# A two-layer attention and Fourier kernel: layer-1 conditioning moved to the gate stage, one reciprocal for both heads, the second low half behind the next maxima

## The chip, the cores and the metric

The kernel runs on one core of one Trainium2 chip. The metric is the device time of one execution in microseconds (us); the figure for a kernel is the median of its timed runs. The engines are TensorE (PE, with its weight loads shown apart as PEld), VectorE (DVE), ScalarE (ACT), GpSimd (POOL) and SyncE (SP), which here only issues DMAs.

## The reference, cut to what matters

Everything is fp32 in and out. Layer 0 is latent attention, layer 1 a Fourier mixing; both are conditioned by a vector.

```python
for i in range(2):
    sh, sc, gt = split(silu(c) @ w_ada[i] + b_ada[i], 3)      # conditioning: three thirds of 1024
    u = rms_norm(h, norm_g[i]) * (1 + sc) + sh
    if i == 0:      # 8 heads, 1024 queries, 1280 keys (256 of them context)
        s = q @ k.T * scale                # q, k from low-rank projections, rotary part added
        p = softmax(s)                     # max, exp, sum over 1280 keys
        y = ((p @ v) * silu(u @ w_gate)) @ w_out0
    else:
        y = (real(fft2(u @ w_z)) * silu(u @ w_gate1)) @ w_out1
    h = h + gt * y
out = rms_norm(h) * final_g
```

So layer 1 needs three vectors of 1024 numbers from `w_ada[1]` (a 1024 x 3072 matrix, 12 MB): `sh` and `sc` before its first product, `gt` at its end.

## The kernel before, in words

To keep fp32 accuracy each operand of a product is split in a high and a low part (`split`: ACT rounds the high part, DVE or POOL subtracts it), and three products are summed (`mm3`, L82).

Stages, by the time of the profiled execution: up to about 95 us the layer-0 conditioning, norms and projections; from 95 to 198 us the **gate stage**; from 198 to 548 us the **attention stage**; then the out-projection of layer 0 with the residual, and from about 600 us layer 1.

*Gate stage.* Nine turns `n`; turn 2 makes the rotary queries (`q_rope`), each other one a chunk of 128 gate columns for two blocks of 512 tokens (`gate_pair`: 2 x 24 matmuls, about 11 us). The weights of a chunk come by DMA on SP's queue into one raw tile `gr`, then ACT writes `gh` and POOL `gl` (L89, L90). Between the turns stand *conditioning thirds* (`ada_third`): a third is sixteen pieces of 128 x 512 of `w_ada`, each loaded by SP into `aw` (four buffers) or `qm` (two) and accumulated by DVE in `aacc` with one scalar_tensor_tensor (L467); POOL clears `aacc` first. `mod_rows` then sums over partitions with four matmuls by ones (L487), ACT copies the result and SP writes it to DRAM (`modd`). Before, two thirds (layer 0's `gt`, layer 1's `gt`) are done here, in turns 0 and 3.

*Attention stage.* 32 steps `i`; `u = i // 4` counts pairs of heads times two token blocks, `p = i % 4` the 128 queries. In a step PE makes the scores of two heads (`scores`, L618 and the last pass L624) in banks 0 to 2 and 3 to 5 of PSUM. `expo`: DVE takes the negated row maximum (L629), ACT the exponential with its sum (L631), into `p32`, which the profile calls `p`. `inverse` makes 1/sum times a power of two on DVE (L635, L636). One step later, in `between`, `quant` writes for each head the high half `hi` on ACT (L642), the low half `lo` on DVE (L644), and SP issues a transposing DMA for each (L643, L645) into `PT`. Two steps later (`LAG`) `pv_step` multiplies `PT` with the values, `values` applies them to the gate. Also in `between` stand preparations: `prep_q` in steps with `p` 0 and 1 (its split is `qh` on ACT, `ql` on DVE, L92 and L93), `prep_pe` (tile `A`), `prep_w`. Layer 1's `sh` and `sc` are accumulated here before: `cond` puts two DVE instructions in each of 16 of the steps 5 to 25, and `mod_rows(1)` in step 28.

The order on PE is written out by hand up to the end of the attention stage, on DVE and ACT in the attention stage; elsewhere a scheduler that simulates the engines decides.

Of the kernel before, what the change touches and what calls it, by code (L numbers as in the profile page):

```python
# [12 lines left out]
ALU = mybir.AluOpType  # L13
# [20 lines left out]
NORM1 = {4: 4, 5: 6}  # L34
TOKENS1 = {6: (0, 1, 2), 7: (3, 4, 5, 6, 7)}

THIRDS = {0: (0, 0, 2), 3: (0, 1, 2)}
SUMS = {5: 0}

COND = [i for i in range(5, 27) if i % 4 != 2][:16]  # L40


def f32(ap):
# [3 lines left out]
def hybrid_kernel(tc, io, out, dbg=None):  # L47
# [384 lines left out]
    close(wq_cm)  # L432


    stb_cm, stb = pool("stb", "right")
    gws.append((stb.tile([P, 8, P], F32R, name="gh1"), stb.tile([P, 8, P], F32R, name="gl1")))

# [17 lines left out]
                cs = slice(e * 512, (e + 1) * 512)  # L455
                split(flat(w[0])[:, cs], flat(w[1])[:, cs], wr[:, cs], scale=gqa[:, e:e + 1])

    def ada_start(layer, j, pl):
        a = pl.tile([P, D], F32, name="aacc", tag="aacc", bufs=2)
        nc.gpsimd.memset(a, 0.0)  # L460
        nc.sync.dma_start(a[0:1, :], io["b_ada"][layer:layer + 1, j * D:(j + 1) * D])
        return a
# [4 lines left out]
        return stt(a[:, cs], w, actc[:, k, 0:1], a[:, cs], ALU.mult, ALU.add)  # L467

    def ada_third(layer, j, qmp=None):
        a = ada_start(layer, j, stb)  # L470
# [11 lines left out]
    def mod_rows(pair, pl):  # L482
# [5 lines left out]
        row = pl.tile([P, 512], F32, name="row", tag="row", bufs=1)  # L488
# [42 lines left out]

    def at(n):
        if n in SUMS:
            mod_rows(SUMS[n], qmp)
        if n in THIRDS:
            pair, layer, j = THIRDS[n]
            thirds.setdefault(pair, []).append(ada_third(layer, j, qmp if n > 2 else None))
# [86 lines left out]
                mm(s[d][:, a:z], qa[u % 2][1][d][x, q], (B1 if d else B2)[x, a:z], start=False, stop=True)  # L624
        return [v[:, 0:1280] for v in s]

    def expo(s):
        mx = atq.tile([P, 4], F32, name="mx", tag="mx", bufs=4)
        nc.vector.tensor_reduce(mx[:, 0:1], s, axis=AX, op=ALU.max, negate=True)  # L629
        p32 = atq.tile([P, 1280], F32, name="p32", tag="p32", bufs=2)  # L630
        act(p32, s, AF.Exp, bias=mx[:, 0:1], accum_out=mx[:, 1:2])  # L631
        return mx, p32

    def inverse(mx, p32):
        nc.vector.reciprocal(mx[:, 2:3], mx[:, 1:2])  # L635
        ts(mx[:, 3:4], mx[:, 2:3], PS14, None, ALU.mult)  # L636

    def quant(mx, p32, PT, half):
        r = mx[:, 3:4]
        hi = ptp.tile([P, 1280], F16, name="phi", tag="phi", bufs=2)  # L640
        lo = ptp.tile([P, 1280], F16, name="plo", tag="plo", bufs=2)
        act(hi, p32, AF.Copy, scale=r)  # L642
        nc.sync.dma_start_transpose(PT[0][:, half], hi)  # L643
        stt(lo, p32, r, hi, ALU.mult, ALU.subtract)  # L644
        nc.sync.dma_start_transpose(PT[1][:, half], lo)  # L645

    PTs, Os = {}, {}

    def pv_step(i, b=7):
        u, p = i // 4, i % 4  # L650
# [18 lines left out]
    gate_chunk(8, 0)  # L669
    for d in range(2):  # L670
        prep_q(0, d, (7, 5)[d])
    close(u_cms[0])
    pt_cm, ptp = pool("ptp2", "left")
    wo0 = [None] * 8
    wraw = [qpe[:, 2 * i:2 * i + 2, :].rearrange("p a c -> p (a c)") for i in range(4)]

    def cond(i, c):
        if i in COND:
            n = COND.index(i)
            w = cnp.tile([P, 512], F32, name="aw", tag="aw", bufs=2)  # L680
            ada_step(1, n // 8, thirds[1][n // 8], n % 8, c, w)

    def between(i):

        u, p = i // 4, i % 4
        if i > 0:
            for d in range(2):
                quant(*es[d], PTs[i - 1], d)
        if 0 < u < 7 and p < 2:
            prep_q(u + 1, p)  # L690
        if i == 2:
            prep_q(1, 1)
        if i == 3:
            prep_pe(1)
        if u > 0 and p == 2:
            values(u - 1, 0)
        if u in (0, 2, 4) and p == 3:
            prep_w(u // 2 + 1)
        if i in (2, 4):
            hs = slice(2 * i - 4, 2 * i)  # L700
            split(wvh[:, hs, :], wvl[:, hs, :], wvr[:, hs, :], scale=gkva)
        if i == 28:
            mod_rows(1, cnp)
        if i >= 29:
            split_wo0(i - 29)
        if i == 31:
            for t in range(2):
                o_split(t, slice(0, 4), wop, gtt)

    ots = [None] * 8  # L710

    def o_split(t, ks, pl, eng, bufs=4):
        if ots[t] is None:
            ots[t] = [None, None]
        sl = slice(t * P, (t + 1) * P)
        for q in range(ks.start // 4, (ks.stop + 3) // 4):
            if ots[t][q] is None:
                ots[t][q] = [pl.tile([P, 4, P], F32R, name=f"o{x}", tag=f"o{x}", bufs=bufs) for x in "hl"]
# [11 lines left out]
    for i in range(16 * 2):  # L730
        u, p = i // 4, i % 4
        if i == 5:
            close(wv_cm)
        if i == COND[0]:
            cn_cm, cnp = pool("cnp", "left")
            thirds[1] = [ada_start(1, j, cnp) for j in range(2)]
        PTs[i] = [ptp.tile([P, 2, NKT, P], F16, name="PT", tag=f"PT{j}", bufs=2) for j in range(2)]
        es = [expo(s) for s in scores(u, p, lambda: between(i))]
        cond(i, 0)
        for e in es:  # L740
            inverse(*e)
        if i < 2:
            gate_chunk(8, 1, range(4 * i, 4 * i + 4))
        if i == 1:
            close(u_cms[1])
            at_cm, atp = pool("atp", "left")
            qa.append(q_tiles(atp, 1))
            scr = atp.tile([P, 8], F32, name="scr")
            wvh, wvl = gws[0]
            wv_cm, wvp = pool("wvp", "left")  # L750
            wvr = wvp.tile([P, NH, P], F32, name="wvr")
            nc.gpsimd.dma_start(wvr, io["wv"])
            prep_q(1, 0, 7)
        if i >= LAG:
            pv_step(i - LAG)
        if 0 < u < 7 and p == 2:
            prep_pe(u + 1)
        if u > 0 and p == 3:
            values(u - 1, 1)
        cond(i, 1)  # L760
        if i == 27:
            for k in range(4):
                nc.gpsimd.dma_start(wraw[k], io["w_out0"][k * P:(k + 1) * P, :])  # L763
        if i == 28:
            close(cn_cm)
            for n, v in ((2, sh1), (3, scr)):
                nc.gpsimd.dma_start(v, modd[n].rearrange("(k p) -> p k", p=P))
            close(cq_cm)
            close(wqk_cm)
            wo_cm, wop = pool("wop", "right")  # L770
            for k in range(3):
                wo0[k] = [(wop.tile([P, 512], F32R, name=f"wh{k}{i_}"), wop.tile([P, 512], F32R, name=f"wl{k}{i_}")) for i_ in range(2)]
    for d in range(2):
        quant(*es[d], PTs[i], d)

    def out_mm(t, bs, ks, wo, first, last, beside=None):
        for k in ks:
# [14 lines left out]
        values(7, d, 4 + d)  # L792
    order2.__exit__(None, None, None)
    order.__exit__(None, None, None)
    for t in range(2):
        o_split(t, slice(4, 8), wop, gtt)
    in_order(stt(sc1, scr, 1.0, ng[:, 8:16], ALU.add, ALU.mult))
    dump("gate", gate)
    close(at_cm)
    close(pt_cm)  # L800
# [66 lines left out]
    for t in range(8):  # L867
        if t >= 2:
            bs = banks(2, 0, 2)
            beside = (lambda k: to_u2(0, n1[0:4], (k,))) if t == 5 else None  # L870
            out_mm(t, bs, range(8), wo0, 0, 7, beside)
        else:
            bs = b0[t]
        if t + 2 < 8:
            xts.append(load_res(t + 2))
            o_split(t + 2, slice(0, 8), wop, gtt)
# [440 lines left out]
```

## Time and profile before

| | us |
|---|---|
| timed runs | 903.22, 904.62, 908.70 |
| median | 904.62 |
| profiled execution | 902.2, its span 900.4 |
| PE busy in the span | 859.6 (95%) |
| DVE / ACT / POOL busy | 584.5 / 405.5 / 274.8 |

Busy time of PE is modelled: matmuls overlap, and a matmul of 512 columns that the profile gives 0.39 us follows its predecessor after 0.23 us. What tells is where PE stood idle and who released it. Times in the views are counted from the start of the span. TensorE runs at one of two levels, 2.4 GHz (granted clock 1.00) and 1.2 GHz (0.50); a value between is a mean over the stretch.

### The profile page before, as it was taken

How to read it: one execution, taken by the hardware profiler on the slowest of the kernel's cores; microseconds unless marked ns; L12 is line 12 of the kernel's file. 1: busy time of each engine (PE TensorE's matmuls, PEld its weight loads, DVE VectorE, ACT ScalarE, POOL GpSimd, SP SyncE). 2: the span in 40 equal slices, each digit the busy share in tenths (PEclk: the TensorE clock that was granted, in tenths of full speed). 3: DMA queues.
4: the chain of work that ended last, by engine and by line, in shares of the span. 5: the costliest groups of instructions: out<-in, count | busy, mean ns of one | idle time of the engine just before them, and what ended most of it. 6: DMA issues, size and time to landing. Idle time of an engine off the chain costs nothing. (4 is left out here: it accounts for less than half of the span.)

```text
span 900.4 us, 13245 instructions
## 1 busy us (share of the span) xinstructions
PE 859.6 (95%) x4963; PEld 709.8 (79%) x4963; DVE 584.5 (65%) x1058; ACT 405.5 (45%) x695; POOL 274.8 (31%) x249
## 2 busy tenths in 40 slices
PE   4999999999899999999999989999999999999996
PEld 2878877887777878787887767888888889988885
DVE  4366887016788888888888753453398736396644
ACT  4465521226656666566655653332343326342211
POOL 2544453200000000000000445764277625256311
PEclk9999999999999999999999999999999999999999
DMA  8921455105678878989989994312044315641221
GB/s 345 333 98 48 135 171 187 48 1 106 112 169 163 177 152 160 176 161 174 207 164 189 170 189 179 118 48 94 28 177 137 127 59 197 215 168 66 93 94 48
DMA packets 200729, 127.90 MB, mean 142 GB/s; under 512 B 171915, under 2 KB 175692, under 8 KB 200408
## 3 DMA queue, kind: packets, MB, share of 16 engines
q1 hardware_dynamic: 198632, 119.10, 51.7%
q0 software_dynamic: 2032, 7.95, 2.9%
q8 instruction: 39, 0.64, 0.3%
q14 instruction: 26, 0.21, 0.1%
HBM read 72.51 MB, written 12.57 MB: 94 GB/s over the span
## 5 line engine op out<-in xcount | busy, mean ns | idle before, releaser
L631 ACT ACTIVATE p<-pb,mx 128x1280 f32<-128x1280 f32 x64 | 85.1, 1329 | 103.4 <-DVE mx L629 103.1
L82 PE MATMUL pb<-PT,n16h 128*128 128x256 f16 x640 | 108.7, 276 | 3.7 <-DMA PT<-plo 3.7
L644 DVE SCALAR_TENSOR_TENSOR plo<-p,mx,phi 128x1280 f16<-128x1280 f32 x64 | 96.7, 1551 | 10.0 <-ACT phi L642 8.6
L629 DVE TENSOR_REDUCE mx<-pb 128x1 f32<-128x1280 f32 x64 | 92.3, 1483 | 8.3 <-PE pb L624 8.0
L82 PE MATMUL pb<-PT,n16l 128*128 128x256 f16 x320 | 88.0, 275 | 0.0
L642 ACT ACTIVATE phi<-p,mx 128x1280 f16<-128x1280 f32 x64 | 83.6, 1358 | 0.1
L82 PEld LDWEIGHTS <-n16h 128*128 128x128 f16 x640 | 60.5, 99 | 15.1 <-issue 8.0
L763 POOL DMA_DIRECT2D qpe<-w_out x4 | 2.1, 532 | 225.9 <-PE pb L596 225.9
L618 PE MATMUL pb<-nkh,qh 128*128 128x512 f32 (+1 forms) x192 | 50.9, 373 | 7.6 <-ACT p L631 7.5
L82 PE MATMUL pb<-wl,oh 128*128 128x512 f32 x128 | 50.1, 392 | 1.1 <-DVE wl L90 1.0
L467 DVE SCALAR_TENSOR_TENSOR aacc<-aw,actc,aacc 128x512 f32<-128x512 f32 x59 | 48.5, 832 | 3.7 <-DMA aw<-w_ada 3.5
L82 PE MATMUL pb<-uh,gh 128*128 128x512 f32 x128 | 50.7, 396 | 0.0
L82 PE MATMUL pb<-ul,gh 128*128 128x512 f32 x128 | 50.0, 391 | 0.0
L82 PE MATMUL pb<-uh,gl 128*128 128x512 f32 x128 | 49.9, 390 | 0.0
L82 PE MATMUL pb<-wh,ol 128*128 128x512 f32 x128 | 49.9, 390 | 0.0
L90 POOL TENSOR_TENSOR ol<-gate,oh 128x512 fp32r<-128x512 f32 (+2 forms) x28 | 41.5, 1493 | 27.6 <-ACT oh L89 26.4
L82 PE MATMUL pb<-wh,oh 128*128 128x512 f32 x128 | 48.7, 397 | 0.0
L618 PE MATMUL pb<-nkh,ql 128*128 128x512 f32 (+1 forms) x192 | 48.3, 360 | 0.0
L618 PE MATMUL pb<-B,A 128*128 128x512 f32 (+1 forms) x192 | 48.1, 359 | 0.0
L618 PE MATMUL pb<-nkl,qh 128*128 128x512 f32 (+1 forms) x192 | 47.7, 357 | 0.0
L618 PEld LDWEIGHTS pb<-nkh,qh 128*128 128x128 f32 x192 | 32.8, 190 | 18.3 <-ACT p L631 13.2
L89 ACT ACTIVATE oh<-gate 128x512 fp32r<-128x512 f32 (+2 forms) x36 | 19.2, 577 | 56.2 <-PE pb L82 50.8
(332 smaller groups left out, 2233.7 us busy)
## 6 DMA issues: line engine op xcount, KB each, us to landing
aw<-w_ada SPq DMA_DIRECT2D x59, 256.0 KB, 3.1
wada<-wada SPq DMA_DIRECT2D x16, 512.0 KB, 8.8
gr<-wg SPq DMA_DIRECT2D x14, 512.0 KB, 3.6
xn<-x SPq DMA_DIRECT2D x8, 512.0 KB, 5.0
xt<-x SPq DMA_DIRECT2D x8, 512.0 KB, 6.3
h1d<-xt SPq DMA_DIRECT2D x8, 512.0 KB, 2.6
wz<-wz SPq DMA_DIRECT2D x8, 512.0 KB, 3.7
ht<-h1d SPq DMA_DIRECT2D x8, 512.0 KB, 6.5
```

The costliest lines, as they stand in the source:

```text
L82: mm(ps, l, r, start=start and i == 0, stop=stop and i == n - 1)
L89: act(hi, src, AF.Copy)
L90: eng(lo, src, f32(hi), ALU.subtract)
L467: return stt(a[:, cs], w, actc[:, k, 0:1], a[:, cs], ALU.mult, ALU.add)
L618: mm(s[d][:, a:z], l[:, q], r[:, a:z], start=i == 0, stop=False)
L629: nc.vector.tensor_reduce(mx[:, 0:1], s, axis=AX, op=ALU.max, negate=True)
L631: act(p32, s, AF.Exp, bias=mx[:, 0:1], accum_out=mx[:, 1:2])
L642: act(hi, p32, AF.Copy, scale=r)
L644: stt(lo, p32, r, hi, ALU.mult, ALU.subtract)
L763: nc.gpsimd.dma_start(wraw[k], io["w_out0"][k * P:(k + 1) * P, :])
```

## The change

1. Conditioning: layer 1's `sh` and `sc` thirds go to turns 5 and 6 of the gate stage (`THIRDS`); `cond` is gone. The accumulators sit in a pool of their own (`smp`). `mod_rows(1)` comes right before the first scores; the result is loaded back by two DMAs on POOL's queue there.
2. Softmax: the maxima and sums of both heads share one tile `mx` of eight columns, and one reciprocal and one scaling serve both heads.
3. Order: the low half of the second head is not made in `between` but after the next step's two maxima (`lows`); `p32` has three buffers.
4. The second half of the first two output tiles (`o_split`, columns 4 to 8) is made after the pool `wo2` has been opened, and `sc1` is finished later.

```diff
-THIRDS = {0: (0, 0, 2), 3: (0, 1, 2)}
+THIRDS = {0: (0, 0, 2), 3: (0, 1, 2), 5: (1, 1, 0), 6: (1, 1, 1)}
 SUMS = {5: 0}
-COND = [i for i in range(5, 27) if i % 4 != 2][:16]
...
-    def expo(s):
-        mx = atq.tile([P, 4], F32, name="mx", tag="mx", bufs=4)
-        nc.vector.tensor_reduce(mx[:, 0:1], s, axis=AX, op=ALU.max, negate=True)
-        p32 = atq.tile([P, 1280], F32, name="p32", tag="p32", bufs=2)
-        act(p32, s, AF.Exp, bias=mx[:, 0:1], accum_out=mx[:, 1:2])
-        return mx, p32
-    def inverse(mx, p32):
-        nc.vector.reciprocal(mx[:, 2:3], mx[:, 1:2])
-        ts(mx[:, 3:4], mx[:, 2:3], PS14, None, ALU.mult)
+    def expo(s, mx, d):
+        nc.vector.tensor_reduce(mx[:, d:d + 1], s, axis=AX, op=ALU.max, negate=True)
+        p32 = ptp.tile([P, 1280], F32, name="p32", tag="p32", bufs=3)
+        act(p32, s, AF.Exp, bias=mx[:, d:d + 1], accum_out=mx[:, 2 + d:3 + d])
+        return p32
+    def inverse(mx):
+        nc.vector.reciprocal(mx[:, 4:6], mx[:, 2:4])
+        ts(mx[:, 6:8], mx[:, 4:6], PS14, None, ALU.mult)
...
         act(hi, p32, AF.Copy, scale=r)
-        nc.sync.dma_start_transpose(PT[0][:, half], hi)
-        stt(lo, p32, r, hi, ALU.mult, ALU.subtract)
-        nc.sync.dma_start_transpose(PT[1][:, half], lo)
+        nc.sync.dma_start_transpose(PT[0][:, d], hi)
+        def low():
+            stt(lo, p32, r, hi, ALU.mult, ALU.subtract)
+            nc.sync.dma_start_transpose(PT[1][:, d], lo)
+        if late:
+            return low
+        low()
...
     for d in range(2):
         prep_q(0, d, (7, 5)[d])
+    mod_rows(1, thirds[1][0][:, 0:512])
+    close(sm_cm)
+    for n, v in ((2, sh1), (3, sc1)):
+        nc.gpsimd.dma_start(v, modd[n].rearrange("(k p) -> p k", p=P))
...
-            for d in range(2):
-                quant(*es[d], PTs[i - 1], d)
+            quant(mx, es[0], PTs[i - 1], 0)
+            lows.append(quant(mx, es[1], PTs[i - 1], 1, True))
...
-        if i == 28:
-            mod_rows(1, cnp)
...
-        es = [expo(s) for s in scores(u, p, lambda: between(i))]
-        cond(i, 0)
-        for e in es:
-            inverse(*e)
+        ss = scores(u, p, lambda: between(i))
+        mx = atq.tile([P, 8], F32, name="mx", tag="mx", bufs=3)
+        es = [expo(s, mx, d) for d, s in enumerate(ss)]
+        while lows:
+            lows.pop()()
+        inverse(mx)
...
-        cond(i, 1)
...
-    for t in range(2):
-        o_split(t, slice(4, 8), wop, gtt)
-    in_order(stt(sc1, scr, 1.0, ng[:, 8:16], ALU.add, ALU.mult))
...
     wo2_cm, wo2 = pool("wo2", "right")
+    opl.append(wo2)
+    for t in range(2):
+        o_split(t, slice(4, 8), gtt)
...
     close(key_cm)
+    in_order(stt(sc1, sc1, 1.0, ng[:, 8:16], ALU.add, ALU.mult))
```

How instructions move, at three places (rows in the order of the engine; x2 is a row twice). First DVE in the attention stage, from the maxima of step 7 to those of step 8: before, then in the changed kernel.

```order
L629 TENSOR_REDUCE mx<-pb 128x1 x2
L467 SCALAR_TENSOR_TENSOR aacc<-aw,actc,aacc 128x512
L635 RECIPROCAL mx<-mx 128x1
L636 TENSOR_SCALAR mx<-mx 128x1
L635 RECIPROCAL mx<-mx 128x1
L636 TENSOR_SCALAR mx<-mx 128x1
L93 SCALAR_TENSOR_TENSOR Ol<-pb,Oh 128x2x128
L665 TENSOR_TENSOR gate<-pb,gate 128x512
L467 SCALAR_TENSOR_TENSOR aacc<-aw,actc,aacc 128x512
L644 SCALAR_TENSOR_TENSOR plo<-p_2601,mx,phi 128x1280
L644 SCALAR_TENSOR_TENSOR plo<-p_2605,mx,phi 128x1280
L93 SCALAR_TENSOR_TENSOR ql_2024<-pb,gks,qh_2023 128x512
```

```order
L627 TENSOR_REDUCE mx<-pb 128x1 x2
L645 SCALAR_TENSOR_TENSOR plo<-p_2584,mx,phi 128x1280
L633 RECIPROCAL mx<-mx 128x2
L634 TENSOR_SCALAR mx<-mx 128x2
L91 SCALAR_TENSOR_TENSOR Ol<-pb,Oh 128x2x128
L669 TENSOR_TENSOR gate<-pb,gate 128x512
L645 SCALAR_TENSOR_TENSOR plo<-p_2676,mx,phi 128x1280
L91 SCALAR_TENSOR_TENSOR ql_2132<-pb,gks,qh_2131 128x512
```

One low half (of the step before) now stands between the maxima and the reciprocal, one is left ahead of the next maxima; the two conditioning instructions and one reciprocal pair are gone.

Second SP's queue in the gate stage, from the last loads of the third in turn 3: before (the last row is the attention stage's first transpose), then in the changed kernel as far as the next gate weights but one.

```order
L466 DMA aw<-w_ada 128x512 x2
L449 DMA gr<-wg 128x1024
L490 DMA modd<-row 4x512
L449 DMA gr<-wg 128x1024 x2
L643 DMA_TRANSPOSE PT<-phi 128x10x128 x2
```

```order
L465 DMA aw<-w_ada 128x512 x4
L448 DMA gr<-wg 128x1024
L465 DMA aw<-w_ada 128x512 x2
L465 DMA qm<-w_ada 128x512
L488 DMA modd<-qm 4x512
L460 DMA aacc<-b_ada 1x1024
L465 DMA qm<-w_ada 128x512
L448 DMA gr<-wg 128x1024
L465 DMA aw<-w_ada 128x512
L460 DMA aacc<-b_ada 1x1024
```

The `gr` loads now stand between loads of `aw` and `qm`, each of which waits for a buffer that DVE has to free. On DVE all 32 new accumulations stand before the split of `wq` that opens the attention stage.

Third ACT at the end of the attention stage, from the last two high halves: before, then in the changed kernel.

```order
L642 ACTIVATE phi<-p_5049,mx 128x1280
L89 ACTIVATE oh<-gate 128x512 x2
L92 ACTIVATE Oh<-pb 128x2x128 x2
L89 ACTIVATE wh_5229<-qpe 128x512
L89 ACTIVATE wh_5231<-qpe 128x512
```

```order
L641 ACTIVATE phi<-p_4951,mx 128x1280
L90 ACTIVATE Oh<-pb 128x2x128 x2
L87 ACTIVATE oh<-gate 128x512 x2
L87 ACTIVATE wh_5130<-qpe 128x512
L87 ACTIVATE wh_5132<-qpe 128x512
```

The two high halves of the output tiles come behind the last attention results, ahead of the weights of the out-projection.

## Rows read from the trace of the kernel before

**Rows 1.** Waits of PE, 195 to 565 us: engine, line, waited for, us, times, longest

```profile
PE pb L618 <- ACT p L631: 7.5, 11, 2.2
```

**Rows 2.** Timeline of PE, attention stage: start us, us, what; in brackets idle before, releaser

```profile
229.29 0.84 PE L618 MATMUL pb<-nkh,qh 128*128 128x512 f32 x3 [2.24 <-ACT p L631]
...
281.49 0.39 PE L82 MATMUL pb<-Oh,gl 128*128 128x512 f32 x1
...
282.14 0.85 PE L618 MATMUL pb<-nkh,qh 128*128 128x512 f32 x3 [0.26 <-ACT p L631]
...
292.95 0.85 PE L618 MATMUL pb<-nkh,qh 128*128 128x512 f32 x3 [0.32 <-ACT p L631]
...
323.57 0.85 PE L618 MATMUL pb<-nkh,qh 128*128 128x512 f32 x3 [0.67 <-ACT p L631]
...
516.79 0.85 PE L618 MATMUL pb<-nkh,qh 128*128 128x512 f32 x3 [1.12 <-ACT p L631]
...
540.51 0.27 PE L82 MATMUL pb<-PT,n16h 128*128 128x256 f16 x1 [3.67 <-DMA PT<-plo]
...
550.27 0.50 PE L82 MATMUL pb<-wl,oh 128*128 128x512 f32 x1 [1.05 <-DVE wl L90]
```

**Rows 3.** Timeline of DVE in step 7: low halves, maxima, second reciprocal

```profile
276.04 3.02 DVE L644 SCALAR_TENSOR_TENSOR plo<-p,mx,phi 128x1280 f16<-128x1280 f32 x2
279.08 2.89 DVE L629 TENSOR_REDUCE mx<-pb 128x1 f32<-128x1280 f32 x2
...
283.52 0.16 DVE L635 RECIPROCAL mx<-mx 128x1 f32<-128x1 f32 x1 [0.62 <-ACT p L631]
```

**Rows 4.** Timeline of DVE before the maxima of step 8

```profile
289.23 0.75 DVE L93 SCALAR_TENSOR_TENSOR ql<-pb,gks,qh 128x512 fp32r<-128x512 f32 x1 [0.84 <-ACT qh L92]
```

**Rows 5.** Timeline of DVE before the maxima of step 2

```profile
224.30 0.74 DVE L93 SCALAR_TENSOR_TENSOR gl<-wvr,cols,gh 128x512 fp32r<-128x512 f32 x1
224.96 2.88 DVE L629 TENSOR_REDUCE mx<-pb 128x1 f32<-128x1280 f32 x2
```

**Rows 6.** Timeline of ACT: first split of wq, and qh of step 2

```profile
190.12 0.72 ACT L89 ACTIVATE wqh<-wqk 128x256 fp32r<-128x256 f32 x2
...
221.82 0.69 ACT L92 ACTIVATE qh<-pb,gks 128x512 fp32r<-128x512 f32 x1
```

**Rows 7.** Windows: length, busy PE PEld DVE ACT POOL, granted clock, DMA share, GB/s

```profile
230.00:235.00 5.00, 5.00 (x22) 4.32 (x21) 3.56 (x5) 4.50 (x7) 0.00 (x0) 0.66 0.36 69
500.00:520.00 20.00, 18.88 (x126) 15.32 (x125) 14.70 (x20) 13.46 (x19) 8.79 (x7) 1.00 0.99 185
```

**Rows 8.** Timeline of DVE, gate stage: conditioning accumulations

```profile
121.90 2.87 DVE L467 SCALAR_TENSOR_TENSOR aacc<-aw,actc,aacc 128x512 f32<-128x512 f32 x1 [0.51 <-DMA aw<-w_ada]
...
135.29 5.27 DVE L467 SCALAR_TENSOR_TENSOR aacc<-aw,actc,aacc 128x512 f32<-128x512 f32 x3
...
149.39 2.73 DVE L467 SCALAR_TENSOR_TENSOR aacc<-aw,actc,aacc 128x512 f32<-128x512 f32 x4
...
153.95 1.54 DVE L467 SCALAR_TENSOR_TENSOR aacc<-aw,actc,aacc 128x512 f32<-128x512 f32 x2
```

**Rows 9.** Timeline of POOL, gate stage: a low half of gate weights

```profile
168.71 2.41 POOL L90 TENSOR_TENSOR gl<-gr,gh 128x1024 fp32r<-128x1024 f32 x1 [8.78 <-ACT gh L89]
```

**Rows 10.** Timeline of SP: sums of layer 0 to DRAM; last low halves' transposes

```profile
158.41 0.59 SPq L490 DMA_DIRECT2D modd<-row  x1
...
532.63 3.30 SPq L645 DMA_TRANSPOSE PT<-plo  x2
```

**Rows 11.** Timeline of PE: first use of wq; sums of layer 1

```profile
195.37 0.39 PE L82 MATMUL pb<-cqh,wqh 128*128 128x512 f32 x1
...
492.05 1.06 PE L487 MATMUL pb<-aacc,ones 128*32 128x512 f32 x8
```

**Rows 12.** Timeline of DVE at the end of attention

```profile
548.94 0.67 DVE L797 SCALAR_TENSOR_TENSOR sc<-scr,cols 128x8 f32<-128x8 f32 x1
```

**Rows 13.** Tile PT, SP, 480 to 545 us

```profile
DMA to landing us min/median/max: 3.4/3.9/5.7
```

More of the change, by code (lines that the diff above doesn't have):

```diff
@@ L432, in hybrid_kernel @@
     close(wq_cm)
+    sm_cm, smp = pool("smp", "right")
     stb_cm, stb = pool("stb", "right")
@@ L456, in gate_w0, with ada_start @@
                 split(flat(w[0])[:, cs], flat(w[1])[:, cs], wr[:, cs], scale=gqa[:, e:e + 1])
-    def ada_start(layer, j, pl):
-        a = pl.tile([P, D], F32, name="aacc", tag="aacc", bufs=2)
+    def ada_start(layer, j):
+        a = smp.tile([P, D], F32, name="aacc", tag="aacc", bufs=2)
         nc.gpsimd.memset(a, 0.0)
@@ L469, in ada_third @@
     def ada_third(layer, j, qmp=None):
-        a = ada_start(layer, j, stb)
+        a = ada_start(layer, j)
         for k in range(8):
@@ L480, in ada_third, with mod_rows @@
         return a
-    def mod_rows(pair, pl):
+    def mod_rows(pair, row):
         b = bank(1, 5, 6, 7) if pair == 0 else pb[:, 6, :]
@@ L487, in mod_rows @@
             mm(b[32 * c:32 * c + 32, :], ones[:, 0:32], a, start=True, stop=True)
-        row = pl.tile([P, 512], F32, name="row", tag="row", bufs=1)
         act(row, b, AF.Copy)
@@ L533, in at @@
         if n in SUMS:
-            mod_rows(SUMS[n], qmp)
+            mod_rows(SUMS[n], qmp.tile([P, 512], F32, name="qm", tag="qm", bufs=2))
         if n in THIRDS:
@@ L625, in scores, with quant @@
         return [v[:, 0:1280] for v in s]
-    def expo(s):
-        mx = atq.tile([P, 4], F32, name="mx", tag="mx", bufs=4)
-        nc.vector.tensor_reduce(mx[:, 0:1], s, axis=AX, op=ALU.max, negate=True)
-        p32 = atq.tile([P, 1280], F32, name="p32", tag="p32", bufs=2)
-        act(p32, s, AF.Exp, bias=mx[:, 0:1], accum_out=mx[:, 1:2])
-        return mx, p32
-    def inverse(mx, p32):
-        nc.vector.reciprocal(mx[:, 2:3], mx[:, 1:2])
-        ts(mx[:, 3:4], mx[:, 2:3], PS14, None, ALU.mult)
-    def quant(mx, p32, PT, half):
-        r = mx[:, 3:4]
+    def expo(s, mx, d):
[6 more added lines that the diff above has]
+        ts(mx[:, 6:8], mx[:, 4:6], PS14, None, ALU.mult)
+    def quant(mx, p32, PT, d, late=False):
+        r = mx[:, 6 + d:7 + d]
         hi = ptp.tile([P, 1280], F16, name="phi", tag="phi", bufs=2)
@@ L642, in quant @@
         act(hi, p32, AF.Copy, scale=r)
-        nc.sync.dma_start_transpose(PT[0][:, half], hi)
-        stt(lo, p32, r, hi, ALU.mult, ALU.subtract)
-        nc.sync.dma_start_transpose(PT[1][:, half], lo)
-    PTs, Os = {}, {}
+        nc.sync.dma_start_transpose(PT[0][:, d], hi)
[5 more added lines that the diff above has]
+        low()
+    PTs, Os, lows = {}, {}, []
     def pv_step(i, b=7):
@@ L675, in hybrid_kernel @@
     wraw = [qpe[:, 2 * i:2 * i + 2, :].rearrange("p a c -> p (a c)") for i in range(4)]
[L677 to L681, printed above, removed]
     def between(i):
@@ L707, in between, with o_split @@
             for t in range(2):
-                o_split(t, slice(0, 4), wop, gtt)
+                o_split(t, slice(0, 4), gtt)
     ots = [None] * 8
-    def o_split(t, ks, pl, eng, bufs=4):
+    opl = []
+    def o_split(t, ks, eng):
         if ots[t] is None:
@@ L717, in o_split @@
             if ots[t][q] is None:
-                ots[t][q] = [pl.tile([P, 4, P], F32R, name=f"o{x}", tag=f"o{x}", bufs=bufs) for x in "hl"]
+                ots[t][q] = [opl[q].tile([P, 4, P], F32R, name=f"o{x}", tag=f"o{x}", bufs=2) for x in "hl"]
             oh, ol = ots[t][q]
@@ L733, in hybrid_kernel @@
             close(wv_cm)
-        if i == COND[0]:
-            cn_cm, cnp = pool("cnp", "left")
-            thirds[1] = [ada_start(1, j, cnp) for j in range(2)]
         PTs[i] = [ptp.tile([P, 2, NKT, P], F16, name="PT", tag=f"PT{j}", bufs=2) for j in range(2)]
-        es = [expo(s) for s in scores(u, p, lambda: between(i))]
-        cond(i, 0)
-        for e in es:
-            inverse(*e)
+        ss = scores(u, p, lambda: between(i))
[4 more added lines that the diff above has]
+        inverse(mx)
         if i < 2:
@@ L747, in hybrid_kernel @@
             qa.append(q_tiles(atp, 1))
-            scr = atp.tile([P, 8], F32, name="scr")
             wvh, wvl = gws[0]
@@ L764, in hybrid_kernel @@
         if i == 28:
-            close(cn_cm)
-            for n, v in ((2, sh1), (3, scr)):
-                nc.gpsimd.dma_start(v, modd[n].rearrange("(k p) -> p k", p=P))
             close(cq_cm)
@@ L770, in hybrid_kernel @@
             wo_cm, wop = pool("wop", "right")
+            opl.append(wop)
             for k in range(3):
@@ L773, in hybrid_kernel @@
     for d in range(2):
-        quant(*es[d], PTs[i], d)
+        quant(mx, es[d], PTs[i], d)
     def out_mm(t, bs, ks, wo, first, last, beside=None):
@@ L875, in hybrid_kernel @@
             xts.append(load_res(t + 2))
-            o_split(t + 2, slice(0, 8), wop, gtt)
+            o_split(t + 2, slice(0, 8), gtt)
         n1.append(residual(t, bs, xts[t]))
```

## The prediction

> **What bounds the kernel now.** I read first who kept PE waiting in the attention stage, since PE works without a gap nearly everywhere else. Eleven waits, 7.5 us together, end with the exponential of the first head [rows 1]: PE can start the next step's scores only when ACT has read the old ones out of PSUM. Then I read PE's timeline for the size of each. The largest are 2.24 us in step 2, 1.12 in step 30, and 0.67, 0.26 and 0.32 in steps 11, 7 and 8 [rows 2]; the row of step 11 stands for step 19 too, that of step 8 for steps 12, 16, 20 and 24, and a wait of 0.98 follows step 4. The other large one is not of that kind: 3.67 us until the last transposed low half has landed, and then 1.05 us for a low half of output weights [rows 2].
>
> Third I asked what held up the exponential. It waits for the maximum, so the question is what DVE did just before the maxima. There are two kinds of step. In step 7 the two low halves run from 276.04 to 279.06 and the maxima follow at 279.08 [rows 3]: the second low half is in their way. In step 8 the maxima come after `ql`, and DVE stood idle 0.84 us before `ql`, waiting for `qh` [rows 4]: there the way leads from PE's preparation over ACT, and no low half lies on it.
>
> A wait costs a little more than its idle time. In step 7 the last matmul before it starts at 281.49 and the next at 282.14, 0.65 us instead of about 0.23, so 0.42 us are lost and not 0.26 [rows 2]: 0.16 more each.
>
> **The change part by part.**
>
> *The low half behind the maxima* gains where it was what the maxima waited for. Steps 7, 11, 19 and 30: 0.26 + 0.67 + 0.67 + 1.12 = 2.72 us, with 4 x 0.16 = 0.64 that makes 3.4. A low half takes half of 3.02 us [rows 3], more than each of these waits, so they go entirely. In steps 8, 12, 16, 20, 24 and 4 `ql` is late for another reason: no gain. Step 2 lies between. After its low halves come `ql` and `gl` (0.74 us at 224.30), then the maxima at 224.96 [rows 5]. Without the second low half `ql` can start when `qh` is done, at 221.82 + 0.69 = 222.5 [rows 6]; two instructions of about 0.7 later the maxima start at 223.9, so 1.0 of 2.24 us goes.
>
> *Clock.* After the 2.24 us the granted clock was 0.66 in 230 to 235 us, a mean of 1.2 and 2.4 GHz; 5 x 0.34 = 1.7 us of work were lost. After 1.12 us idle the stretch 500 to 520 kept 1.00 [rows 7]. With 1.2 us left in step 2 I take the nearer row: no fall, gain 1.7 us. The bounds are 0 and 1.7.
>
> *What becomes late next.* The second low half now ends 4.45 us after its step's maxima begin (2.89 for the maxima, then 1.55), and its transpose lands 3.4 to 5.7 us after issue [rows 3, 13]: 7.9 to 10.2 us. `pv_step` needs it when the next step's scores end, about 10.2 us after the maxima in most steps (279.08 to 289.9 in step 7), under 9 in step 30. In most steps that is covered; in step 30 a wait of up to 1.2 us is possible, but PE then waits for the final transpose anyway.
>
> *One reciprocal for both heads.* DVE already stood idle 0.62 us until the second exponential's sum was there [rows 3], and the first high half follows that exponential on ACT. So it starts at most one reciprocal and one scaling (0.16 us each) later, which nothing waits for except at the end. It saves 64 tiny instructions off the path: nothing.
>
> *The end of attention.* The last transposes were issued from 532.63 over 3.30 us [rows 10]. Before them now lie the later reciprocal (0.3 us) and, close ahead on SP's queue, the transpose of step 30's second low half (1.65 us by the same row) in a stretch where the DMA engines are 0.99 busy [rows 7]. Bounds: 0.3 and 2.0 us of loss. I take 0.8, since SP would be free again at about the time when the first high half of step 31 is ready. On the other side `sc1` (0.67 us, [rows 12]) no longer stands before the first `wl` for which PE waited 1.05: gain 0.6. The output tiles' high halves now delay the weights of POOL's part by some 2.5 us, but those products were moved back on PE as well: between 0 and 1.5 us of loss, I take 0.
>
> *Conditioning.* Removing 32 DVE instructions of some 0.74 us from attention gains nothing by itself: they stood after the maxima or before a low half that waited for ACT. `mod_rows(1)` costs PE 1.06 us at 492 [rows 11] and will cost that at 198: nothing. What must be found is room in the gate stage. Accumulation can start when layer 0's sums have left: `modd` is issued at 158.41 [rows 10], the bias row of `b_ada` is now queued behind it and behind a load more, and a transfer takes 2 to 3 us: 162.4. Undisturbed, four take 2.73 us [rows 8], 0.68 each, so 32 take 21.8. Three `gl` of 2.41 us on POOL fall in [rows 9], and one accumulation beside such an instruction took 2.87 us [rows 8], 2.1 more: 6.3. That ends at 190.5. `wq` is split from 190.12 on ACT [rows 6], then on DVE, and PE first uses it at 195.37 [rows 11]; with 1.4 us for the two splits the accumulations may end as late as 194. So: no cost, with 3.5 us to spare. If that cover is gone, PE waits before the first scores. On SP's queue the gate weights now wait behind loads that need a free buffer, by 1 to 4 us; they were in place some 7 us before PE's turn for them (two chunks of 11 us alternate), so that is covered too.
>
> **Sum.** -3.4 - 1.0 - 1.7 + 0.8 - 0.6 = -5.9 us. The profiled execution took 902.2, so 896.3 by its own measure; it stands 2.4 below the median of the runs, 904.6, and the median of the changed kernel should be 904.6 - 5.9 = **898.7**. Own range with the bounds of the terms: 896 to 903.
>
> **Rivals.**
>
> *The gate stage has no room (slower).* For it: the third of turn 3 took sixteen accumulations from 135.29 to 153.95 + 1.54 = 155.49 us [rows 8], 1.26 each, because of POOL and waits for loads. At that pace 32 end at 162.4 + 40.4 = 202.8, and PE waits 8.8 us from 194; with a fall of the clock as in step 2, 1.7 more. Net -5.9 + 10.5 = +4.6: **909.2**. It decides from 0.99 us per instruction, and the gain is used up at 1.17. Against it: six loads are already in when the accumulations start, and the three `gl` come eleven us apart. Chance 0.22, half of it with only a part of the price.
>
> The page GPSIMD Engine Reference of the Trainium skill, section Key points, says that POOL shares its SBUF interfaces with DVE and gets in the way of DVE instructions with two SBUF inputs; `aacc` and `aw` are two. The 2.87 us against 0.68 agree [rows 8]. Counting by that rule all five POOL instructions of the stretch, the two clearings too, my estimate would be 5 x 2.1 = 10.5 instead of 6.3 and an end at 194.7, just past the limit.
>
> *The end shrinks.* With the conditioning loads gone the DMA engines might deliver the last low half in time: 3.67 us and the clock's 1.7 behind it. For: share 0.99 in 500 to 520. Against: those loads had ended by step 25, so what fills that stretch stays. Net -5.9 - 5.4: **893.4**. Chance 0.12.
>
> *The low half is late for `pv_step`.* Short steps only, 1.2 us each in two or three of them: **901.5**. Chance 0.10; it would need landings near 5.7 us.
>
> *No effect.* If ACT, not the low half, is what the maxima's successors wait for, only the `wl` term is left: **904**. Against it stands the gap of 0.02 us in step 7 [rows 3]. Chance 0.06.
>
> My forecast keeps 0.50. A change of 1% (9 us) is about what a measurement can tell from none: below 895.6 lie most of the shrinking end and the best of the forecast, 0.16; above 913.7 only the worst of the gate stage, 0.08; within, 0.76. The range of 8 in 10 leaves out half of the shrinking end and the dearer half of the gate stage: 894 to 908.
>
> **What would show it.** Right: PE's waits for the exponential fall from eleven and 7.5 us to seven and about 3.8; the granted clock stays 1.00 around step 2; the last accumulation ends near 190, and PE goes into the sums of layer 1 without idle time; the wait for the last transpose grows to about 4.5 us. Wrong: a wait of PE for `wqh`, `wql` or `aacc` near 195 us; a wait for `PT` in the middle steps; the maxima of steps 7, 11 and 19 still right behind another DVE instruction.

## The result and the profile after

The changed kernel took 894.85 us (median of 893.51 to 896.11), the kernel before beside it 905.81: a ratio of 0.9882, 95% interval 0.9855 to 0.9909. Measured again with the experiments: 895.64 against 903.77, ratio 0.9909, 0.9886 to 0.9932. The forecast was 898.7 in a range of 894 to 908. The profiled execution took 895.71 (span 893.9), 6.5 less than that of before.

First the waits of PE, 195 to 565 us, beside [rows 1]: engine, line, waited for, us, times, longest.

```profile
PE pb L80 <- DMA PT<-plo: 4.0, 3, 1.6
PE pb L616 <- ACT p L629: 3.5, 7, 1.3
PE pb L80 <- DMA PT<-phi: 2.0, 1, 2.0
PE pb L80 <- DVE wl L88: 0.5, 1, 0.5
```

The waits for the exponential fell from eleven to seven and by 4.0 us, as forecast. Waits for the transposed halves (`PT`) are now the larger sum, 6.0 us. PE's timeline shows where; these rows answer to [rows 2].

```profile
239.27 0.85 PE L616 MATMUL pb<-nkh,qh 128*128 128x512 f32 x3 [1.32 <-ACT p L629]
...
250.65 0.84 PE L616 MATMUL pb<-nkh,qh 128*128 128x512 f32 x3 [0.91 <-ACT p L629]
...
439.90 0.27 PE L80 MATMUL pb<-PT,n16h 128*128 128x256 f16 x1 [1.54 <-DMA PT<-plo]
...
482.10 0.27 PE L80 MATMUL pb<-PT,n16h 128*128 128x256 f16 x1 [1.57 <-DMA PT<-plo]
...
534.92 0.27 PE L80 MATMUL pb<-PT,n16h 128*128 128x256 f16 x1 [1.96 <-DMA PT<-phi]
...
536.08 0.27 PE L80 MATMUL pb<-PT,n16h 128*128 128x256 f16 x1 [0.88 <-DMA PT<-plo]
...
545.25 0.50 PE L80 MATMUL pb<-wl,oh 128*128 128x512 f32 x1 [0.45 <-DVE wl L88]
```

Steps 7, 11, 19 and 30 no longer wait, and neither does step 2. New are 1.32 us in step 3 and two waits for a low half, in the last steps of two units (23 and 27; by `LAG` the halves are those of steps 21 and 25). At attention's end PE waits 1.96 + 0.88 instead of 3.67 us, and 0.45 instead of 1.05 for the first weights.

The larger part of why step 2 waits no more stands on ACT: first its rows before, then after (start, us, what, idle before).

```profile
226.52 1.28 ACT L631 ACT_TABLE_LOAD   x1 [3.41 <-DVE mx L629]
227.82 1.33 ACT L631 ACTIVATE p<-pb,mx 128x1280 f32<-128x1280 f32 x1
```

```profile
223.95 0.72 ACT L90 ACTIVATE gh<-wvr,cols 128x512 fp32r<-128x512 f32 x1
224.69 1.28 ACT L629 ACT_TABLE_LOAD   x1
226.94 1.33 ACT L629 ACTIVATE p<-pb,mx 128x1280 f32<-128x1280 f32 x1 [0.97 <-DVE mx L627]
```

Before, the table load of the exponential stood behind the wait for the maximum, on the path. Now it stands ahead of that wait. The Trainium skill (ScalarE: Activation LUTs, section What ACT_TABLE_LOAD costs) gives about 1283 ns for such a load, and both rows agree (1.28 us).

In the gate stage the accumulations on DVE, answering to [rows 8], POOL's part, [rows 9], and the first split of `wq` on ACT, [rows 6]:

```profile
163.23 1.42 DVE L466 SCALAR_TENSOR_TENSOR aacc<-aw,actc,aacc 128x512 f32<-128x512 f32 x2 [7.38 <-DMA aacc<-b_ada]
...
170.00 2.02 DVE L466 SCALAR_TENSOR_TENSOR aacc<-aw,actc,aacc 128x512 f32<-128x512 f32 x1 [1.25 <-DMA aw<-w_ada]
...
184.01 3.60 DVE L466 SCALAR_TENSOR_TENSOR aacc<-aw,actc,aacc 128x512 f32<-128x512 f32 x2 [1.17 <-DMA aw<-w_ada]
...
193.00 1.54 DVE L466 SCALAR_TENSOR_TENSOR aacc<-aw,actc,aacc 128x512 f32<-128x512 f32 x2
```

```profile
169.06 2.41 POOL L88 TENSOR_TENSOR gl<-gr,gh 128x1024 fp32r<-128x1024 f32 x1 [5.74 <-ACT gh L87]
184.55 2.50 POOL L88 TENSOR_TENSOR gl<-gr,gh 128x1024 fp32r<-128x1024 f32 x1 [13.08 <-PE pb L80]
```

```profile
192.95 0.72 ACT L87 ACTIVATE wqh<-wqk 128x256 fp32r<-128x256 f32 x2 [2.38 <-DVE aacc L466]
```

They ran from 163.23 to 194.54 us, 0.98 each, and PE did not wait. Hardly any room was left: the low parts of `wq` were ready at 195.21 and PE first used one at 196.18.

### The profile page after: what moved, and what is told of

It is laid out like the page before. It is cut to its first block, busy times and chain, and to the rows that moved or that the text cites. A ratio compares the mean times of both kernels' runs of the same rounds, so it can differ in the third digit from the quotient of the medians.

```text
span 893.9 us, 13137 instructions
## 1 busy us (share of the span) xinstructions
PE 856.5 (96%) x4963; PEld 710.3 (79%) x4963; DVE 589.3 (66%) x994; ACT 409.4 (46%) x695; POOL 275.1 (31%) x249
## 5 line engine op out<-in xcount | busy, mean ns | idle before, releaser
L645 DVE SCALAR_TENSOR_TENSOR plo<-p,mx,phi 128x1280 f16<-128x1280 f32 x64 | 98.9, 1547 | 25.0 <-ACT phi L641 24.8
L466 DVE SCALAR_TENSOR_TENSOR aacc<-aw,actc,aacc 128x512 f32<-128x512 f32 x49 | 44.1, 919 | 16.5 <-DMA aw<-w_ada 8.5
```

## The experiments

Medians, with the ratio to before and its 95% interval. They come from three sessions of four, four and three kernels, in which before itself took 903.99, 903.77 and 902.56 us; so kernels of different sessions are compared by their ratios.

| kernel | us | ratio |
|---|---|---|
| conditioning only | 898.59 | 0.9946 (0.9925 to 0.9967) |
| and a third buffer | 897.55 | 0.9930 (0.9907 to 0.9952) |
| change, low half not late | 901.33 | 0.9973 (0.9954 to 0.9992) |
| change, two reciprocals | 894.45 | 0.9898 (0.9875 to 0.9921) |
| before, output halves moved | 900.12 | 0.9959 (0.9944 to 0.9974) |
| change, weights later | 894.24 | 0.9895 (0.9876 to 0.9915) |
| change, weights and gate later | 890.70 | 0.9857 (0.9837 to 0.9877) |
| change again | 895.64 | 0.9909 (0.9886 to 0.9932) |
| change, weights truly later | 893.41 | 0.9898 (0.9882 to 0.9915) |
| change, all loads later | 890.61 | 0.9874 (0.9854 to 0.9893) |
| change, four buffers | 908.32 | 1.0061 (1.0045 to 1.0078) |

**Conditioning only.** The change with its softmax lines undone; of the diff only the order of the low halves is shown, the joint reciprocal and the third buffer go back too:

```diff
-            lows.append(quant(mx, es[1], PTs[i - 1], 1, True))
+            for d in range(2):
+                quant(*es[d], PTs[i - 1], d)
```

> The change with its softmax part undone: each head has its own reciprocal again, the second low half comes before the next maxima, and the exponentials rotate through two buffers. What is left is the conditioning in the gate stage and the moved ends. Theory A (the prediction's): the conditioning gives nothing but the 0.6 us at the first weights after attention; PE still waits eleven times and some 7.5 us for the exponential, 2.2 us of it in step 2, and the time is 0.5 to 2 us below before. Theory B (the larger part of the gain comes from DVE and DMA work that left attention): over 4 us below before, and the waits for the exponential fall below 5 us.

Ten waits for the exponential, 7.6 us, 2.24 of it in step 2: theory A's picture in the middle. Yet the time fell by 5.4 us, as B said, though not by the shorter waits that B asked for. What the profile shows of the gain is at the end of attention:

```profile
538.72 0.27 PE L80 MATMUL pb<-PT,n16h 128*128 128x256 f16 x1 [2.02 <-DMA PT<-plo]
546.22 0.50 PE L80 MATMUL pb<-wl,oh 128*128 128x512 f32 x1 [0.47 <-DVE wl L88]
```

The wait for the last low half is 1.65 us shorter, that for the weights 0.58, and the clock did not fall behind them (1.00 in 530 to 545 us). Neither theory had named this place.

**Output halves moved.** To find the cause, the kernel before with only this (shortened; the tiles of this half come from the second pool too):

```diff
-    for t in range(2):
-        o_split(t, slice(4, 8), wop, gtt)
     in_order(stt(sc1, scr, 1.0, ng[:, 8:16], ALU.add, ALU.mult))
...
     wo2_cm, wo2 = pool("wo2", "right")
+    opl.append(wo2)
+    for t in range(2):
+        o_split(t, slice(4, 8), wop, gtt)
```

> The kernel before with one thing of the change: the second half of the first two output tiles is split after attention's end (its tiles from the second pool), so that POOL's low halves of it (3.5 us, behind 2.3 of waiting for ACT) no longer stand ahead of the 512 KB load of gtb on POOL's queue. Conditioning and softmax stay as before. Theory A (the end shrank in the kernel with the conditioning alone because this load goes 6 us earlier, out of the way of the last low halves' transposes): PE's last wait for a low half falls from 3.67 to about 2.0 us, the clock does not fall behind it, 3 to 4 us below before. Theory B (the end shrank because conditioning work or its loads left attention): wait still 3.5 to 4, within 1 us of before.

POOL's timeline, first before, then this kernel:

```profile
530.39 3.54 POOL L90 TENSOR_TENSOR ol<-gate,oh 128x512 fp32r<-128x512 f32 x2 [2.33 <-ACT oh L89]
533.89 0.56 POOL L494 DMA_DIRECT2D gtb<-modd  x1
```

```profile
529.73 0.54 POOL L494 DMA_DIRECT2D gtb<-modd  x1
545.05 2.55 POOL L90 TENSOR_TENSOR ol<-gate,oh 128x512 fp32r<-128x512 f32 x2 [14.79 <-ACT oh L89]
```

and its PE:

```profile
540.70 0.27 PE L82 MATMUL pb<-PT,n16h 128*128 128x256 f16 x1 [2.18 <-DMA PT<-plo]
549.44 0.50 PE L82 MATMUL pb<-wl,oh 128*128 128x512 f32 x1 [1.68 <-DVE wl L90]
```

Theory A: two low halves ahead of a 512 KB load on POOL's queue had put it beside the last transposes. With that order gone the wait fell from 3.67 to 2.18 us without any change to the conditioning, no fall of the clock followed, and the time fell by 3.7 us. The POOL work that left this place is not the reason by itself: DVE's last two low halves took 3.02 us with and without it, and ACT's last two high halves 2.61. Of the 5.4 us of the kernel above some 1.2 remain for the conditioning itself and `sc1`, less than the intervals resolve. The 0.6 at the weights comes with the rest of the change; here that wait is longer, 1.68.

**A third buffer.** The conditioning kernel with

```diff
-        p32 = atq.tile([P, 1280], F32, name="p32", tag="p32", bufs=2)
+        p32 = ptp.tile([P, 1280], F32, name="p32", tag="p32", bufs=3)
```

> As the kernel with the conditioning alone, but the exponentials rotate through three buffers instead of two. Theory A: with two buffers the exponential waits for two engines' semaphores and one of the waits stands ahead of the table load (in the profile of before the load began at 226.52 behind 3.41 us of idle for the maximum, in that of after at 224.69, before the maximum); with three it waits for DVE alone, the load of 1.28 us goes ahead of that wait, and PE's wait in step 2 falls from 2.24 to about 1.0 us, the clock no longer falls behind it, 1.3 to 3 us below the kernel with two buffers. Theory B (the load went ahead because ACT was free earlier, as the low half had moved): no change against two buffers, wait in step 2 still 2.2 us.

ACT around the table load, then PE in steps 2 and 3:

```profile
225.78 1.28 ACT L629 ACT_TABLE_LOAD   x1
229.12 1.33 ACT L629 ACTIVATE p<-pb,mx 128x1280 f32<-128x1280 f32 x1 [2.06 <-DVE mx L627]
```

```profile
230.59 0.85 PE L616 MATMUL pb<-nkh,qh 128*128 128x512 f32 x3 [0.89 <-ACT p L629]
241.84 0.85 PE L616 MATMUL pb<-nkh,qh 128*128 128x512 f32 x3 [1.70 <-ACT p L629]
```

Theory A: the low halves are where they were, and the load has left the path. With two buffers the first exponential's list of waits holds a semaphore of DVE and one of ACT, with three that of DVE alone. The wait in step 2 is 1.35 us shorter and the clock did not fall behind it (1.00 in 225 to 245 us, where the conditioning kernel has 0.91: another 1.7), but step 3 now waits 1.70 where it had not waited: over half of the gain is due back one step later. The ratio moved by 0.0016, less than these intervals resolve, so the 1.3 to 3 us of theory A are not shown in the time.

**Low half not late.**

```diff
-            lows.append(quant(mx, es[1], PTs[i - 1], 1, True))
+            quant(mx, es[1], PTs[i - 1], 1)
```

> The change with the second low half back in front of the next maxima; the joint reciprocal and the third buffer stay. Theory A (the late half gives 3.4 us in steps 7, 11, 19 and 30 and takes 3.0 in steps 23 and 27, where the transposed low half came 1.54 and 1.57 us late): the two waits for the low half are gone, those of steps 7, 11, 19 and 30 are back, each 0.3 larger than before because the joint reciprocal lets the first high half start 0.3 later; the time is within 2 us of the change. Theory B (the late half is the whole gain): 5 us or more above the change. Theory C (it is a loss by now): 2 us or more below it.

By the time theory B's figure, 6 us above the change, but not its reason, as the next kernel shows. Fifteen waits for the exponential, 10.2 us; step 11, and step 30 with twice its wait of before:

```profile
326.57 0.85 PE L616 MATMUL pb<-nkh,qh 128*128 128x512 f32 x3 [0.84 <-ACT p L629]
...
521.75 0.85 PE L616 MATMUL pb<-nkh,qh 128*128 128x512 f32 x3 [2.44 <-ACT p L629]
```

Behind that wait and behind one of 2.02 in step 3 the granted clock fell (columns: length, busy PE PEld DVE ACT POOL, granted clock, DMA share, GB/s):

```profile
241.00:251.00 10.00, 9.16 (x42) 7.25 (x43) 4.95 (x7) 6.35 (x9) 0.00 (x0) 0.83 0.48 108
520.00:530.00 10.00, 8.25 (x40) 6.63 (x41) 6.29 (x8) 7.81 (x11) 3.14 (x2) 0.83 0.67 165
```

So 10 x 0.17 = 1.7 us of work were lost at each of the two places, which theory A had not counted. This kernel differs from the one with the third buffer only by the joint reciprocal and the tile that both heads then share, and is 3.8 us slower: without the late half the joint reciprocal costs.

**Two reciprocals.**

```diff
-        nc.vector.reciprocal(mx[:, 4:6], mx[:, 2:4])
-        ts(mx[:, 6:8], mx[:, 4:6], PS14, None, ALU.mult)
+        for m in mx:
+            nc.vector.reciprocal(m[:, 2:3], m[:, 1:2])
+            ts(m[:, 3:4], m[:, 2:3], PS14, None, ALU.mult)
```

> The change with a reciprocal and a scaling for each head again, on tiles of their own; the low half stays late. Theory A: the joint reciprocal holds the first high half back (0.51 us between the second exponential's end and the first high half's start on ACT, of which 0.21 idle, against 0.26 before), so with two reciprocals the chain high half, low half, maxima runs 0.2 to 0.3 us earlier: PE's waits of 1.32 in step 3, 0.91 in step 4 and 0.26 in five steps of a first quarter shrink by that, 1 to 2.5 us below the change. Theory B (the 64 small instructions that the joint one saves count on DVE): 1 us or more above the change. Theory C: no difference, within 0.5 us.

Theory C: 0.9898 lies between the change's two ratios. Step 3 waits 1.13 instead of 1.32, the other waits for the exponential are as they were. With the late half the joint reciprocal neither gives nor costs anything that shows.

This kernel differs from the one with the third buffer by the late half alone (and by how its small tiles rotate), so the two give its price: 894.45 against 897.55 us, 3.1 less, with intervals that overlap. From the first scores to the wait for the weights behind attention their profiles take the same time, first with the third buffer (546.01 - 200.65), then here (545.32 - 199.98):

```profile
200.65 0.85 PE L616 MATMUL pb<-nkh,qh 128*128 128x512 f32 x3
546.01 0.50 PE L80 MATMUL pb<-wl,oh 128*128 128x512 f32 x1 [0.47 <-DVE wl L88]
```

```profile
199.98 0.85 PE L616 MATMUL pb<-nkh,qh 128*128 128x512 f32 x3
530.12 0.40 PE L80 MATMUL pb<-PT,n16h 128*128 128x256 f16 x1 [2.93 <-DMA PT<-plo]
545.32 0.50 PE L80 MATMUL pb<-wl,oh 128*128 128x512 f32 x1 [0.47 <-DVE wl L88]
```

The late half took away the waits of steps 7, 11, 19 and 30 (2.5 us there) and of step 2 (0.89), and brought 1.39 and 1.38 in steps 23 and 27, 2.93 instead of 2.05 at the end, and a fall of the clock behind that (0.83 in 525 to 535 us). So by itself it gives nothing in these profiles and about 3 us by the medians; the 6 us above hold the price of the joint reciprocal too.

**Weights later, and truly later.** First the loads moved in the program:

```diff
-        if i == 27:
-            for k in range(4):
-                nc.gpsimd.dma_start(wraw[k], ...)
+        if i in (24, 28):
+            for k in ((0, 1) if i == 24 else (2, 3)):
+                nc.sync.dma_start(wraw[k], ...)
```

> The change with the four loads of 512 KB of output weights, which POOL issued at 432.8 and 474.9, two at a time, taken to SP's queue behind steps 24 and 28. Theory A (the low half of steps 22 and 26 was late in the short step behind it because these loads held up the transposes): the waits of 1.54 and 1.57 us for the low half are gone, about 3 us below the change. Theory B (the late half alone is too late for a short step): both waits stay, no difference.

Inconclusive, for the loads did not move. First POOL's loads and SP's transpose of the late half in the change, then SP's timeline here:

```profile
432.79 1.06 POOL L762 DMA_DIRECT2D qpe<-w_out  x2 [215.15 <-PE pb L594]
```

```profile
433.30 1.49 SPq L646 DMA_TRANSPOSE PT<-plo  x1
```

```profile
432.92 0.82 SPq L762 DMA_DIRECT2D qpe<-w_out  x2
433.84 1.61 SPq L646 DMA_TRANSPOSE PT<-plo  x1
```

The scheduler placed them where their space comes free, straight ahead of the late half; the waits were 0.85 and 0.94. So they were tied to the late halves:

```diff
+            if late:
+                in_order(op)
...
-                nc.sync.dma_start(wraw[k], ...)
+                in_order(nc.sync.dma_start(wraw[k], ...))
```

> The change with the four loads of output weights on SP's queue and held in order with the late low halves' transposes, so that they leave about 452 and 494 us; in the kernel with the weights later they had still left at 432.9, the moment at which their space came free. Theory A (these loads hold up the low halves of the short steps): the waits in steps 23 and 27, 1.6 us each in the change, are gone or below 0.3, some 3 us below the change. Theory B (the late half alone is too late for a step of 9.3 us): 0.8 us or more is left in each.

SP's loads, then PE's waits for a low half before the last:

```profile
455.38 1.05 SPq L764 DMA_DIRECT2D qpe<-w_out  x2
493.76 1.05 SPq L764 DMA_DIRECT2D qpe<-w_out  x2
```

```profile
507.15 0.27 PE L80 MATMUL pb<-PT,n16h 128*128 128x256 f16 x1 [0.64 <-DMA PT<-plo]
...
516.43 0.28 PE L80 MATMUL pb<-PT,n16h 128*128 128x256 f16 x1 [0.22 <-DMA PT<-plo]
```

Theory A: the waits in steps 23 and 27 are gone. Two smaller ones came near the second pair's new place; the ratio cannot be told from the change's.

**The gate's load last.**

```diff
-    gtb0 = gt_load(0, xtp)
+    gtb0 = xtp.tile([P, D], F32, name="gtb0")
+    nc.sync.dma_start(gtb0, modd[0:1, :].broadcast_to([P, D]))
```

> As the kernel with the weights later, and the 512 KB of gtb issued by SP behind the last transposes instead of by POOL at 524.8, ahead of them. Theory A (every large load beside the last transposes costs at the end): PE's waits for the last high and low halves, 1.96 and 0.88 us in the change, shrink by 0.5 to 1.5 us together, and the clock may not fall behind them (1.7 more). Theory B (those waits are the chain from the last exponential to the transposes and hold without any load): no difference to the kernel with the weights later.

PE at attention's end:

```profile
531.85 0.27 PE L80 MATMUL pb<-PT,n16h 128*128 128x256 f16 x1 [0.36 <-DMA PT<-phi]
532.98 0.28 PE L80 MATMUL pb<-PT,n16h 128*128 128x256 f16 x1 [0.86 <-DMA PT<-plo]
```

Theory A: 1.22 us of waits instead of 2.84 (2.55 with the weights later), no fall of the clock behind them, 890.7 us (the low halves in steps 23 and 27, with their loads where the first try had left them, still cost 1.03 and 1.14). All its runs (890.2 to 891.1) lie below all of the change's in the same rounds (893.2 to 897.8): it beats both kernels.

> The change itself once more, on the chip and in the rounds of the three others. If its first ratio of 0.988 holds: 892 to 897 us, and PE's waits as in its first profile (1.3 in step 3, 1.5 and 1.6 for low halves in steps 23 and 27, 2.8 at the end), but for where the clock falls.

That was the run beside it; it came as expected, but for 1.46 + 0.87 us at the end. The clock did not fall there this time, but behind the wait of 1.62 us in step 23. And with both loads held back:

> As the kernel with the weights truly later, and the load of gtb on SP's queue behind the last transposes. If both loads matter and their effects add: waits in steps 23 and 27 as in the kernel with the weights truly later, the last waits for the high and low halves about 0.4 and 0.9 us (as with weights and gate later, against 1.5 to 2.0 and 0.9 in the change), no fall of the clock at attention's end, 888 to 891 us. If the weights' new places collide with other transposes: a new wait for a low half between 452 and 510, and no gain over 890.7.

890.61 us: the last wait is 0.86, but a wait of 0.85 came at 507 us, and nothing is gained over 890.7.

**Four buffers.**

```diff
-                if qmp is not None and (2 * k + i) % 3 == 2:
+                if qmp is not None and layer == 0 and (2 * k + i) % 3 == 2:
```

> The change with layer 1's conditioning loads in the gate stage through four buffers instead of six. Theory A (the rival of the prediction: the gate stage has hardly any room, the last accumulation ends 0.5 to 1 us before PE is held up): with four buffers a load of 3.5 us and an accumulation of 0.9 give 1.1 us an instruction, 32 of them end about 198.5 or later, PE waits 3 to 6 us before the first scores for the splits of wq, and the time is 3 to 8 us above the change. Theory B (the loads are not what sets the pace, POOL is): the last accumulation ends within 1 us of the change's 194.5, no wait of PE, no difference in time.

PE before the first scores, and the stretch around it:

```profile
204.84 0.80 PE L80 MATMUL pb<-cqh,wql 128*128 128x512 f32 x1 [7.74 <-DVE wql L88]
```

```profile
200.00:212.00 12.00, 7.16 (x23) 4.26 (x24) 6.77 (x11) 3.43 (x6) 0.00 (x0) 0.57 0.18 59
```

Theory A, dearer than expected: 1.22 us an accumulation (from 165.4 to 204.4 us, 12.8 of them waiting for loads), 7.74 us of waiting and 12 x 0.43 = 5.2 us of work lost to the clock. At 0.98 the stage hides everything, at 1.22 the change is slower than before.

## Why the prediction was right, and where not

The number held, at the edge of the range (two of the four runs lie below 894); the sum held less well. It had 5.9 us where the runs give 8 to 11: the middle of attention gave less than forecast and its end more. Part by part, as ratios to before: the moved output halves alone 0.9959, with the conditioning 0.9946, with the third buffer 0.9930, with the late half 0.9898, with the joint reciprocal 0.9882 and 0.9909. The first step (3.7 us) is clear of the noise, and it was forecast as nothing; the softmax part as a whole, from 0.9946 on, is too (3 to 6 us); its single parts are not. So that the number held is in part luck.

- *Waits of steps 7, 11, 19, 30, -3.4: the waits right, the gain not shown.* All gone, and back without the late half; but the waits that the late half brought in steps 23 and 27 and at the end take them back in the profiles (two reciprocals against the third buffer).
- *Step 2, -1.0, and the clock, -1.7: right in sum, wrong in the way.* The wait went wholly. The table load, which I had not looked at, took 1.35 of it (third buffer alone: 2.24 to 0.89), the late half the other 0.89, near the 1.0 of the forecast. Step 3 asked 1.32 back: its maxima follow `A`, which on ACT stands behind the high halves, which follow the exponentials of step 2 (DVE stood idle 0.79 us before its part of `A`, for ACT's). So steps 2 and 3 are bound together. Net 0.9. The granted clock around it stayed 1.00 (row of 225 to 245 us below, beside [rows 7]).
- *"In most steps that is covered": failed for steps 23 and 27.* This is the rival of the late low half (0.10, 1.2 us each): 1.54 and 1.57 us. What it lacked was the cause, a pair of 512 KB loads beside the transpose, shown by holding them back. PE went on 6.6 us after the transpose's issue (433.30 to 439.90), past the 5.7 that the rival asked for.
- *End of attention, +0.8: failed, sign and cause.* I costed the moved output halves by the weights that they delay and took 0; on POOL's queue they had been ahead of a load. The wait fell by 0.8 us net in this profile, by 1.5 where only that order changed. This is the shrinking end (0.12), not by the conditioning loads that I had named. `wl`, -0.6, was right.
- *Joint reciprocal, 0: right only behind the late half.* Without it it costs 3.8 us.
- *Room in the gate stage: right by 1 us instead of 3.5.* Start 163.2 for 162.4, end 194.5 for 190.5. Only two `gl` fell in, and the accumulations beside them (one of 2.02 us, two of 3.60 together) cost some 3.4 where I had 6.3. The others took 0.73 instead of 0.68 each, 1.5 in all. What I had at nothing was waiting for loads, in this view of DVE's waits, 162 to 195 us (the wait for the bias row is before the start):

```profile
DVE aacc L466 <- DMA aw<-w_ada: 4.3, 5, 1.3
```

By the GPSIMD Engine Reference of the Trainium skill, section Key points, POOL contends with DVE instructions that have two SBUF inputs, and the three slow accumulations agree. Counted by it for five instructions the end came out at 194.7, near the measured one by chance: the loads made up the difference, as the four buffers show.

The pair of profiles differs by 6.5 us, the runs by 8 to 11. Part is the draw: before's profiled 902.2 stands at the lower end of its runs (898.8 to 908.7 over the sessions). A further part is where the clock falls, some 1.7 us each time. In the profile before it fell in step 2 and at attention's end; in the one after it fell at attention's end too and at 60 to 80 us (0.91), in work that the change leaves as it was, so that the 1.7 us of step 2 do not show in this pair. The second profile of the change has the fall at 60 to 80 us, none at attention's end, and one behind the wait of 1.62 us in step 23. So a late low half can cost the clock as well, which neither the sum nor its rival had counted. Two stretches of the profile after, then one of the second profile of the change:

```profile
225.00:245.00 20.00, 18.68 (x127) 15.44 (x124) 15.69 (x19) 14.24 (x19) 0.00 (x0) 1.00 0.68 129
530.00:545.00 15.00, 11.96 (x61) 8.78 (x58) 2.63 (x5) 4.28 (x9) 2.91 (x3) 0.89 0.69 186
```

```profile
440.00:450.00 10.00, 9.81 (x54) 7.93 (x54) 5.64 (x7) 5.64 (x7) 0.00 (x0) 0.83 0.91 163
```

A third part lies in layer 1, where no term looked: near 774 us PE waited 1.1 us for the tables `tabh` and `tabl` in the profile before and not in the two of the change, while the other kernels show anything up to 2.1 there with nothing edited. What else makes the runs scatter stays open.

## What to carry to other kernels

When an instruction is moved on an in-order queue, ask what stood behind it, loads above all: here that was worth more than what the move was costed for. A wait that goes is gain only up to the next bound of the same chain, so cost neighbouring steps together. Work put into a covered stage is free up to an edge; work out the pace with the loads' latency and the number of buffers, since past the edge the clock is lost as well.

## What was not expected of the hardware

- A table load went ahead of the wait of the exponential that needs it or stood behind it, 1.28 us on the path or not, with the number of buffers that its output rotates through: behind with two (in three kernels), ahead with three.
- A pair of 512 KB loads beside a transpose cost PE some 1.5 us, twice in the middle, and a single one as much at the end (3.67 to 2.18); held back, the pairs cost nothing there, and 0.64 and 0.22 us where the second met other transposes.
- How long PE idled did not decide alone whether the clock fell. At attention's end it fell after 1.43 and 0.90 us with four buffers (0.89 in 545 to 560 us) and after 1.96 and 0.88 in the change, but not after 1.46 and 0.87 in the change again (1.00), nor after 2.02, 2.05 and 2.18 in three other kernels. In step 23 it fell after 1.62 us and not after 1.54. In step 2 it fell after 2.24 (once 2.23) in all three profiles that have that wait.
